# The second layer's query projection as two seven-product pairs, planned together with the feed-forward part before it

## The chip, the cores and the metric

The kernel runs on one core of a Trainium2 chip. The metric is the device time of one execution in microseconds. A core has TensorE (PE, matrix products), VectorE (DVE), ScalarE (ACT), GpSimd (POOL) and SyncE (SP, which here issues the DMAs). Each engine takes its own instructions in order, and semaphores make one wait for another.

## The reference

A trunk of two layers on 256 rows of 2048 columns, in float32. Only the parts around the change:

```python
D_MODEL = 2048; SEQ = 256; N_HEADS = 16; HEAD_DIM = 128; D_FF = 8192
...
    for l in range(N_A):                       # one layer: attention, then
        ...
        h = h + sq_relu_mlp(h, mlp_norm_g[layer], mlp_w1[layer], mlp_w2[layer])
    kv = rms_norm(h, kv_norm_g) @ kv_w         # shared keys and values
    k_sh, v_sh = jnp.split(kv, [D], axis=-1)
    k_sh = rms_norm(k_sh.reshape(B, S, H, Dh), kv_k_g)
    for l in range(N_B):                       # one layer
        u = rms_norm(h, b_norm_g[l])
        q = rms_norm((u @ b_w_q[l]).reshape(B, S, H, Dh), b_q_g[l])
        o = chunked_relbias_attention(q, k_sh, v_sh, b_rel[l])
        h = h + o.reshape(B, S, D) @ b_w_out[l]
        h = h + sq_relu_mlp(h, mlp_norm_g[layer], mlp_w1[layer], mlp_w2[layer])
```

`b_w_q` is 2048x2048: the query projection is `u @ b_w_q`, 256x2048 by 2048x2048.

## The kernel before

**Products.** A float32 product is made of three passes in a rounded type: each operand x is split into a high part hi and a rest lo = x - hi, and hi·hi, lo·hi and hi·lo are added up in PSUM (`passes`, L461, L463, L465: L461 and L463 read the weights' hi, with the activations' high and low part, L465 the weights' lo). The weights are split on the chip: a unit is a tile of 128x1024 weights, two input tiles (of 128) by 512 columns; ACT makes its hi (L217), DVE its lo (L218). There are three hi and three lo buffers, and four for the raw weights, so the splits run at most two or three units ahead of TensorE. A plain unit is 12 matmuls: two input tiles, two blocks of 128 rows, three passes.

**Panels.** An output panel is 512 columns by the 256 rows, and takes 8 units (u = 0 to 7) over the 16 input tiles. `stage` computes the first two panels side by side, and the others one after another. After each plain unit `run_fill` issues one slot of a list of side work (`fill`), to which the steps that follow from a panel are added: `add_fill` puts its first list into the next slot.

**Seven-product pairs.** In the feed-forward parts, two panels (a, the left, and b, the right) form a `Pair`. Its first four (or, in a wide pair, six) input tiles and two row blocks and two panels are taken as a 2x2 by 2x2 block product and multiplied in seven products instead of eight (`form_products`). The seven items are called "11", "T3", "T2", "T1", "21", "T4", "22" (`Form`); the names are those of the four weight blocks w11, w12, w21, w22 and of four sums of them: T3 = w22 + w12, T2 = T3 + w11, T4 = w21 + T2, T1 = w12 + w11. `bring` (L798) loads a block by DMA into a room of the tags "k" and "v"; `make` (L802, L810) makes a sum on DVE; in wide pairs `put` makes T1 and T4 by an adding DMA. `prepare` does so at set distances (units left until the pair begins), given by `when`, for ("12", "22", "21", "11", "T3", "T1"). The sums of the activations that the items "T3", "T2", "T1" and "22" need are made by `sums` (L284 to L294). An item of 1024 columns is six matmuls. In PSUM the parts are put together by copies on ACT (L890, L896, L912) and by DVE (L892 after the third item, L900 after the pair's own a2 or a3).

**The plan.** `plan_mlp` writes the order of all pairs of a feed-forward part: `Pair.plan` puts the four first items between the last three units b5, b6, b7 of the pair before, and the other three between its own units, as `own` says ("F" is an item). The feed-forward part of layer 1 has 16 pairs: for each of four chunks of 2048 hidden columns two pairs of the first and two of the second weight matrix. Its very first pair is 1024 wide with the order "early"; the others are wide.

**Around the query projection.** The residual stream h is held in SBUF by rows. When a panel n of h is done (L582), `next_x` queues: sums of squares (`rows`, L411), a turn of 32x32 blocks (L329), a DMA out to memory and back (`carry`, L339, L345) that completes the turn, and `split_turned`: scaling by the norm's gain (L305), hi (L308) and lo (L309). That gives a quarter of the projection's input, four tiles. In which slot each step stands is listed in `LONG` (this stage) and `SHORT`. The same turned rows, flipped, are later split again for the K/V projection (`again`). The queries are normed per head (`head_norm`: L538, L541, L545, L546, then L550 and L329), carried out and back, and scaled (`scale_q`, L572).

The query projection is one `stage` of four plain panels, after the feed-forward part:

```python
    turns[0] = 1 - turns[0]
    stage(xb, evs, (1 - turns[0], 2))
```

The order of instructions on DVE, ACT, TensorE and SP is the written order (`keep_order`).

Of the kernel before, what the change touches and what calls it, by code (L numbers as in the profile page):

```python
# [9 lines left out]
F32 = mybir.dt.float32  # L10
# [39 lines left out]
def trunk(ctx: ExitStack, tc: tile.TileContext, xT, xr, gs, hg, bf, wgate, w_in, w_oa, w1a, w1fa, w1sa, w2fa, w2sa,  # L50
# [69 lines left out]
    class Pair:  # L120
# [9 lines left out]

        def plan(self, rest):
            made = [self.items(f"f{i} h{i}" if self.wide else f"f{i}") for i in range(7)]
            own = {"early": "a2 F a3 F b2 F b3 a4 b4 a5 a6 a7", "wide": "a3 F b3 F a4 F b4 a5 a6 a7", "ahead": "a3 F a4 F a5 F a6 a7 b3 b4"}[self.order].split()
            plan = made[0] + rest[:1] + made[1] + rest[1:2] + made[2] + rest[2:] + made[3]
            n = 4
            for i in own:
                if i == "F":
                    plan += made[n]
                    n += 1
                else:  # L140
                    plan += self.items(i)
            return plan, self.items("b5 b6 b7")

    def plan_mlp(w1, w1f, w1s, w2f, w2s, tail):
# [12 lines left out]

        close = (7, 5, 1, 4, 3, 2)
        for c in range(NCH):
            for q in range(2):  # L160
                i = 2 * c + q
                order = "ahead" if i else "early"
                when = (25, 20, 9, 15, 10, 8) if not i else (9, 7, 1, 5, 3, 2) if i == 1 else close
                add(w1, w1f, w1s, i, WIDE1, order, when)
            for q in range(2):
                i = 2 * c + q
                add(None, w2f, w2s, i, WIDE2, "wide", close)
        plan, rest = [], [(tail, 0, u) for u in range(KT // UA - 3, KT // UA)]
# [9 lines left out]
    n_out = w_oa.shape[0] - 3  # L178
    queue(w_oa, n_out)
    tail_a = Tail(w_oa, n_out - 5)  # L180
    plan_a = plan_mlp(w1a, w1fa, w1sa, w2fa, w2sa, tail_a)
    queue(w_qb, w_qb.shape[0])
    for i in range(w_kv.shape[0]):
        units.append(w_kv[i])
    queue(w_ob, n_out)
# [163 lines left out]
    def turned(name=None):  # L349
        z = qkv.tile([P, GH * T], F32, name="z")  # L350
        return (z, qkv.tile([P, GH * T], F32, name=name, tag=name, bufs=2)) if name else z


    LONG = ((0, 1, 3, 5, 9, 10), (0, 1, 3, 5, 11, 12), (0, 1, 3, 5, 9, 10), (0, 1, 3, 5, 9, 10))
    SHORT = ((3, 1, 2, 3, 6, 7, 9, 9, 10), (4, 2, 3, 5, 10, 11, 13, 14, 22), (1, 2, 3, 4, 9, 10), (0, 0, 1, 2, 4, 5))

    def next_x(n, r2, stats, which, into, kept=None, fs=None, then=None):
        add_h = residual(n, r2)
        zt, way = [], []
        fs = fs if n < 2 else None  # L360
        at = (LONG if kept is not None else SHORT)[n]

        def use(flipped=False, which=which, into=into):
            t = zt[1].rearrange("p (i k b c) -> p k b i c", i=4, k=GH, b=NB)
            if flipped:
                t = t[:, :, :, ::-1, ::-1]
            return split_turned(t, n, which, into, fs)
# [24 lines left out]
        return f  # L392
# [409 lines left out]
    def make(p, name):  # L802
        t = p.t
        if name == "T3":
            t[name] = prob.tile([P, 9 * 3 * P], F32, name="wT3", tag="p", bufs=1) if p.order == "early" else room("bias", "wT3")
# [17 lines left out]
    def mlp(plan, x, Sx, st, last):  # L823
        base = turns[0]
        hids = [[] for _ in range(NCH)]
        Sh = [[] for _ in range(NCH)]
# [42 lines left out]
        def open_pair(p):  # L869
            m = pairs.index(p)  # L870
            c, second, r = m // 4, m % 4 >= 2, m % 2
            p.x, p.fs = (hids[c], Sh[c]) if second else (x, Sx)
            p.ps = [acc_pair(base), acc_pair(2 if p.third else 1 - base)]
            if second:
# [43 lines left out]
    xkv = []  # L918
    again = [steps(lambda n=n: kept[n](True, 2, xkv)) for n in range(NG)]
    add_fill([[], [], [st2.both], [], [st2.flip]])  # L920
# [136 lines left out]
```

## Time and profile before

| | |
|---|---|
| time, median of 3 runs | 2087.33 us (2087.27 to 2087.92) |
| the profiled execution's own time | 2087.66 us |
| its span | 2085.9 us |
| TensorE busy | 2080.1 us (100%), 9242 matmuls |
| DVE busy | 1614.3 us (77%) |
| ACT busy | 1247.4 us (60%) |
| DMA | 538.85 MB, mean 258 GB/s |

In a row of a group stand the line, the engine, the operation, output and inputs with their shapes, the count, the busy time and the mean of one in ns, and after a bar the idle time ahead of them and who ended it. In a row of the timeline stand the start and the length in us, the engine, the line, the operation, and how many instructions were merged (xN); in brackets the idle time before and who ended it. A row of a windows answer gives a stretch, its length, then busy time and count for PE, PEld, DVE, ACT and POOL, the granted clock, the DMA share and GB/s.

### The profile page before, as it was taken

What the parts mean: (1) busy time and instruction counts of PE and PEld (TensorE: products, weight loads), DVE (VectorE), ACT (ScalarE), POOL (GpSimd) and SP (SyncE); (2) the same over time, 40 slices, a digit from 0 to 9 for tenths busy, and PEclk for the clock granted to TensorE, in tenths of its full rate; (3) what the DMA queues carried; (4) which work ended last, traced back from release to release, by engine and by line L of the source; (5) the groups of instructions that cost most, each with busy time, mean ns of one, the idle gap of its engine ahead of it and who ended that gap; (6) DMA issues with size and microseconds to landing.
All of it is one profiled execution on the core that took longest, in us unless ns stands there. A gap on an engine that the chain in (4) does not pass through costs nothing.

```text
span 2085.9 us, 26322 instructions
## 1 busy us (share of the span) xinstructions
PE 2080.1 (100%) x9242; PEld 1724.1 (83%) x9242; DVE 1614.3 (77%) x1944; ACT 1247.4 (60%) x1623; POOL 110.6 (5%) x123
## 2 busy tenths in 40 slices
PE   9999999999999999999999999999999999999999
PEld 7888888888888888888888888888888888888887
DVE  6767666888788888788777577778987887888786
ACT  6545455766566566557675455456765665665664
POOL 1101000000000000000001001000000000000000
PEclk9999999999999999999999999999999999999999
DMA  8787788798798799789778777788987987997895
GB/s 287 247 257 243 224 260 267 248 284 274 237 284 270 250 281 293 219 278 300 232 238 271 221 232 240 245 261 271 274 266 254 270 282 242 288 273 246 273 289 166
DMA packets 181207, 538.85 MB, mean 258 GB/s; under 512 B 36801, under 2 KB 72017, under 8 KB 181073
## 3 DMA queue, kind: packets, MB, share of 16 engines
q1 hardware_dynamic: 171248, 484.69, 68.9%
q0 software_dynamic: 9824, 52.46, 13.6%
q8 instruction: 73, 1.20, 0.2%
q14 instruction: 62, 0.50, 0.1%
HBM read 497.20 MB, written 39.87 MB: 257 GB/s over the span
## 4 chain that ended last, share of the span: by engine, by line
PE 99%; DMA 0%; DVE 0%; SPq 0%; ACT 0%; DVEq 0%; issue 0%
PE acc L461 26%; PE acc L463 26%; PE acc L465 26%; PE s L465 6%; PE s L461 6%; PE s L463 6%; PE s L604 1%; PE po L634 1%; PE s L603 0%; PE po L635 0%; DMA raw<-in_w_in 0%; PE s L726 0%; DVE lo L218 0%; ACT hi L217 0%; DVE acc L900 0%; DVE h L582 0%
## 5 line engine op out<-in xcount | busy, mean ns | idle before, releaser
L218 DVE TENSOR_TENSOR lo<-raw,hi 128x1024 fp32r<-128x1024 f32 (+1 forms) x582 | 705.2, 1215 | 233.6 <-ACT hi L217 218.4
L217 ACT ACTIVATE hi<-raw 128x1024 fp32r<-128x1024 f32 (+1 forms) x582 | 611.2, 1051 | 273.5 <-PE acc L463 208.9
L461 PE MATMUL acc<-hi,act 128*128 128x512 f32 x2122 | 584.0, 393 | 0.8 <-ACT hi L217 0.7
L463 PE MATMUL acc<-hi,act 128*128 128x512 f32 x2122 | 575.0, 389 | 0.0
L465 PE MATMUL acc<-lo,act 128*128 128x512 f32 x2122 | 574.4, 389 | 0.0
L463 PEld LDWEIGHTS acc<-hi,act 128*128 128x128 f32 x2122 | 398.1, 188 | 83.8 <-DVE act L272 0.5
L465 PEld LDWEIGHTS acc<-lo,act 128*128 128x128 f32 x2122 | 398.3, 188 | 82.8
L461 PEld LDWEIGHTS acc<-hi,act 128*128 128x128 f32 x2122 | 396.2, 188 | 81.7 <-ACT hi L217 1.2
L217 ACT ACTIVATE hi<-w 128x1024 fp32r<-128x1024 f32 x130 | 137.2, 1056 | 106.1 <-DMA w<-in_w1fa 21.0
L218 DVE TENSOR_TENSOR lo<-w,hi 128x1024 fp32r<-128x1024 f32 x130 | 157.8, 1214 | 26.1 <-ACT hi L217 26.0
L218 DVE TENSOR_TENSOR lo<-wT,hi 128x1024 fp32r<-128x1024 f32 x94 | 114.6, 1219 | 65.3 <-ACT hi L217 65.1
L217 ACT ACTIVATE hih<-w 128x512 fp32r<-128x512 f32 x120 | 75.2, 626 | 75.2 <-PE acc L463 64.3
L217 ACT ACTIVATE hi<-wT 128x1024 fp32r<-128x1024 f32 x94 | 99.1, 1055 | 27.0 <-ACT hi L217 8.9
L461 PE MATMUL s<-hi,act 128*128 128x512 f32 x392 | 106.2, 389 | 0.0
L463 PE MATMUL s<-hi,act 128*128 128x512 f32 x392 | 106.1, 389 | 0.0
L465 PE MATMUL s<-lo,act 128*128 128x512 f32 x392 | 106.1, 389 | 0.0
L217 ACT ACTIVATE hih<-wT 128x512 fp32r<-128x512 f32 x90 | 56.4, 627 | 72.2 <-PE acc L463 60.9
L218 DVE TENSOR_TENSOR loh<-w,hih 128x512 fp32r<-128x512 f32 x120 | 82.3, 686 | 19.0 <-ACT hih L217 19.0
L463 PEld LDWEIGHTS s<-hi,act 128*128 128x128 f32 x392 | 73.6, 188 | 15.3
L465 PEld LDWEIGHTS s<-lo,act 128*128 128x128 f32 x392 | 73.6, 188 | 15.3
L461 PEld LDWEIGHTS s<-hi,act 128*128 128x128 f32 x392 | 73.5, 188 | 15.2
L218 DVE TENSOR_TENSOR loh<-wT,hih 128x512 fp32r<-128x512 f32 x90 | 62.0, 688 | 20.5 <-ACT hih L217 20.2
(213 smaller groups left out, 1901.5 us busy)
## 6 DMA issues: line engine op xcount, KB each, us to landing
raw<-in_w_in SPq DMA_DIRECT2D x96, 512.0 KB, 4.9
raw<-in_w2sa SPq DMA_DIRECT2D x80, 512.0 KB, 5.8
raw<-in_w2sb SPq DMA_DIRECT2D x80, 512.0 KB, 5.8
raw<-in_w1sa SPq DMA_DIRECT2D x70, 512.0 KB, 5.9
raw<-in_w1sb SPq DMA_DIRECT2D x70, 512.0 KB, 6.0
raw<-in_w_kv SPq DMA_DIRECT2D x64, 512.0 KB, 4.5
turn<-z SPq DMA_DIRECT2D x60, 512.0 KB, 5.0
w<-in_w2fa SPq DMA_DIRECT2D x32, 768.0 KB, 7.2
```

Source lines behind the costliest of these rows:

```text
L217: S.activation(hi[:, c], raw[:, c], AF.Copy)
L218: V.tensor_tensor(lo[:, c], raw[:, c], hi[:, c].bitcast(F32), op=ALU.subtract)
L461: TE.matmul(ps[:, cols], xh, cut(hi, j), start=first, stop=False, **kw)
L463: TE.matmul(ps[:, cols], xl, cut(hi, j), start=False, stop=False, **kw)
L465: TE.matmul(ps[:, cols], xh, cut(lo, j), start=False, stop=last, **kw)
L604: TE.matmul(s[:, P : 3 * P], q[:, a, P:T], k[:, a], start=True, stop=True)
L634: TE.matmul(po[:, :T], v[:, 0, a * P : (a + 1) * P], pT[:, :2], start=True, stop=False)
```

## The change

- The query projection becomes two more pairs at the end of the plan of layer 1's feed-forward part (`plan_mlp(..., w_qb)`, and `more` in `mlp`). Both are 1024 wide, with the new orders "query" and "", and take seven products on the first four input tiles. So the first four items of the first stand between the last three units of the feed-forward part. Their weights are laid out for that (`_cols_a(..., True)`).
- All four weight sums are made on DVE; T3 (and T2, in its place) gets a third of a new tile `query` from the pool `prob`; the other two thirds hold the turned parts three and four of the input.
- The activations' sums are made for part one (`fs=Sb`, `thirds=False`).
- `LONG` is rewritten: with fewer slots between the steps.
- The flipped parts for K/V, the row statistics and the head norms (now deferred for all groups but the first) get other slots.

```diff
@@ Pair.plan
-            own = {"early": "a2 F a3 F b2 F b3 a4 b4 a5 a6 a7", "wide": "a3 F b3 F a4 F b4 a5 a6 a7", "ahead": "a3 F a4 F a5 F a6 a7 b3 b4"}[self.order].split()
+            own = {"early": "a2 F a3 F b2 F b3 a4 b4 a5 a6 a7", "wide": "a3 F b3 F a4 F b4 a5 a6 a7", "ahead": "a3 F a4 F a5 F a6 a7 b3 b4",
+                   "query": "a2 F b2 F a3 F b3 a4 b4 a5 a6 a7", "": "a2 F a3 F a4 F a5 a6 a7 b2 b3 b4"}[self.order].split()
@@ plan_mlp
+        if more is not None:
+            for q in range(2):
+                add(more, None, None, q, (), "" if q else "query", close if q else (7, 5, 1, 4, 2, 1))
...
-    plan_a = plan_mlp(w1a, w1fa, w1sa, w2fa, w2sa, tail_a)
-    queue(w_qb, w_qb.shape[0])
+    plan_a = plan_mlp(w1a, w1fa, w1sa, w2fa, w2sa, tail_a, w_qb)
@@ next_x
-    LONG = ((0, 1, 3, 5, 9, 10), (0, 1, 3, 5, 11, 12), (0, 1, 3, 5, 9, 10), (0, 1, 3, 5, 9, 10))
+    def query_room(i):
+
+        if not query:
+            query.append(prob.tile([P, 9 * 3 * P], F32, name="query", tag="p", bufs=1))
+        return query[0][:, i * UN : i * UN + UN]
+
+    LONG = ((0, 1, 2, 4, 6, 7, 8, 9, 9), (0, 1, 2, 4, 6, 7), (0, 0, 1, 3, 5, 6), (0, 0, 1, 3, 5, 6))
...
-        fs = fs if n < 2 else None
+        fs = fs if n < 1 + thirds else None
...
-            zt.extend(turned("s" if kept is not None and n >= 2 else "q"))
+            zt.extend((turned(), query_room(n - 1)) if kept is not None and n >= 2 else turned("q"))
@@ make
         if name == "T3":
+            if p.order in ("query", ""):
+                t[name] = query_room(0)
...
@@ open_pair
+            if c == NCH:
+                p.x, p.fs, evacs = more
+                p.evac = evacs[2 * r : 2 * r + 2]
...
@@ after the plan
-    mlp(plan_a, x1, S1, st1, lambda n, r2: next_x(n, r2, st2, 3, xb, kept))
...
-    slots = {4: 0, 5: 0, 11: 1, 12: 1, 13: 2, 14: 2, 21: 3, 22: 3}
-    add_fill([[again[slots[i]]] if i in slots else [] for i in range(23)])
+    slots = {7: 0, 8: 0, 11: 1, 12: 1, 13: 2, 14: 2, 18: 3, 19: 3}
+    def next_b(n, r2):
+        f = next_x(n, r2, st2, 3, xb, kept, fs=Sb, thirds=False)
...
-                box["lq"], box["f"] = lq, head_norm(lambda: st2, z, lq, apart=(0, 2, None, None)[g])
+                box["lq"], box["f"] = lq, head_norm(lambda: st2, z, lq, apart=0 if g else None)
...
-                add_fill([[]] * (7 + (2, 4, 0, 0)[g]) + [[lambda: qs.append(scale_q(box["lq"], 1, g))]])
+                add_fill([[]] * (9 if g else 7) + [[lambda: qs.append(scale_q(box["lq"], 1, g))]])
-    turns[0] = 1 - turns[0]
-    stage(xb, evs, (1 - turns[0], 2))
+    mlp(plan_a, x1, S1, st1, next_b, (xb, Sb, evs))
```

More of the change, by code (lines that the diff above doesn't have):

```diff
@@ L142, in plan, with plan_mlp @@
             return plan, self.items("b5 b6 b7")
-    def plan_mlp(w1, w1f, w1s, w2f, w2s, tail):
+    def plan_mlp(w1, w1f, w1s, w2f, w2s, tail, more=None):
         pairs = []
@@ L351, in turned, with next_x @@
         return (z, qkv.tile([P, GH * T], F32, name=name, tag=name, bufs=2)) if name else z
-    LONG = ((0, 1, 3, 5, 9, 10), (0, 1, 3, 5, 11, 12), (0, 1, 3, 5, 9, 10), (0, 1, 3, 5, 9, 10))
+    query = []
+    def query_room(i):
[3 more added lines that the diff above has]
+    LONG = ((0, 1, 2, 4, 6, 7, 8, 9, 9), (0, 1, 2, 4, 6, 7), (0, 0, 1, 3, 5, 6), (0, 0, 1, 3, 5, 6))
     SHORT = ((3, 1, 2, 3, 6, 7, 9, 9, 10), (4, 2, 3, 5, 10, 11, 13, 14, 22), (1, 2, 3, 4, 9, 10), (0, 0, 1, 2, 4, 5))
-    def next_x(n, r2, stats, which, into, kept=None, fs=None, then=None):
+    def next_x(n, r2, stats, which, into, kept=None, fs=None, then=None, thirds=True):
         add_h = residual(n, r2)
         zt, way = [], []
-        fs = fs if n < 2 else None
+        fs = fs if n < 1 + thirds else None
         at = (LONG if kept is not None else SHORT)[n]
@@ L366, in use @@
                 t = t[:, :, :, ::-1, ::-1]
-            return split_turned(t, n, which, into, fs)
+            return split_turned(t, n, which, into, None if flipped else fs)
         def turn():
-            zt.extend(turned("s" if kept is not None and n >= 2 else "q"))
+            zt.extend((turned(), query_room(n - 1)) if kept is not None and n >= 2 else turned("q"))
             for b in range(NB):
@@ L804, in make @@
         if name == "T3":
-            t[name] = prob.tile([P, 9 * 3 * P], F32, name="wT3", tag="p", bufs=1) if p.order == "early" else room("bias", "wT3")
+            if p.order in ("query", ""):
+                t[name] = query_room(0)
+            else:
+                t[name] = prob.tile([P, 9 * 3 * P], F32, name="wT3", tag="p", bufs=1) if p.order == "early" else room("bias", "wT3")
         else:
@@ L821, in prepare, with mlp @@
                 (bring if name[0] != "T" else put if p.adds and name == "T1" else make)(p, name)
-    def mlp(plan, x, Sx, st, last):
+    def mlp(plan, x, Sx, st, last, more=None):
         base = turns[0]
@@ L871, in open_pair @@
             c, second, r = m // 4, m % 4 >= 2, m % 2
-            p.x, p.fs = (hids[c], Sh[c]) if second else (x, Sx)
+            if c < NCH:
+                p.x, p.fs = (hids[c], Sh[c]) if second else (x, Sx)
             p.ps = [acc_pair(base), acc_pair(2 if p.third else 1 - base)]
-            if second:
+            if c == NCH:
+                p.x, p.fs, evacs = more
+                p.evac = evacs[2 * r : 2 * r + 2]
+            elif second:
                 p.evac = [(last if c == NCH - 1 else residual)(2 * r + q, st.r2) for q in range(2)]
@@ L916, in trunk, with g @@
     st2, xb, kept = RowStats("b"), [], []
-    mlp(plan_a, x1, S1, st1, lambda n, r2: next_x(n, r2, st2, 3, xb, kept))
-    xkv = []
+    xkv, Sb = [], []
     again = [steps(lambda n=n: kept[n](True, 2, xkv)) for n in range(NG)]
-    add_fill([[], [], [st2.both], [], [st2.flip]])
-    slots = {4: 0, 5: 0, 11: 1, 12: 1, 13: 2, 14: 2, 21: 3, 22: 3}
-    add_fill([[again[slots[i]]] if i in slots else [] for i in range(23)])
+    slots = {7: 0, 8: 0, 11: 1, 12: 1, 13: 2, 14: 2, 18: 3, 19: 3}
+    def next_b(n, r2):
+        f = next_x(n, r2, st2, 3, xb, kept, fs=Sb, thirds=False)
+        def g(b, ps):
+            f(b, ps)
+            if (n, b) == (NG - 1, NB - 1):
+                add_fill([[], [], [st2.both], [], [st2.flip]])
+                add_fill([[again[slots[i]]] if i in slots else [] for i in range(20)])
+        return g
     qs, evs = [], []
@@ L1035 @@
         "w_kv": _cols_a(kv),
-        "w_qb": _cols_a(i["b_w_q"][0]),
+        "w_qb": _cols_a(i["b_w_q"][0], True),
         "w_ob": _cols_a(i["b_w_out"][0]),
```

## The prediction

> **What bounds the kernel now.** I read the page first: the head, the busy shares, the chain that ended last, and the costliest groups.
>
> ```profile
> span 2085.9 us, 26322 instructions
> PE 2080.1 (100%) x9242; PEld 1724.1 (83%) x9242; DVE 1614.3 (77%) x1944; ACT 1247.4 (60%) x1623; POOL 110.6 (5%) x123
> PE 99%; DMA 0%; DVE 0%; SPq 0%; ACT 0%; DVEq 0%; issue 0%
> L463 PE MATMUL acc<-hi,act 128*128 128x512 f32 x2122 | 575.0, 389 | 0.0
> ```
>
> TensorE bounds it: 100% busy, 99% of the chain. So a matmul that goes is time that goes, and any wait that TensorE gets is time that comes. I next read the timeline of TensorE through the query projection, and where this kernel, at the end of the feed-forward part before it, already lets TensorE wait.
>
> ```profile
> 1046.81 1.07 PE L461 MATMUL acc<-hi,act 128*128 128x512 f32 x4
> 1047.71 1.07 PE L463 MATMUL acc<-hi,act 128*128 128x512 f32 x4
> ...
> 1134.15 1.07 PE L461 MATMUL acc<-hi,act 128*128 128x512 f32 x4
> ...
> 1012.84 0.39 PE L465 MATMUL acc<-loh,Sh 128*128 128x512 f32 x1
> ...
> 1017.60 0.39 PE L465 MATMUL acc<-loh,act 128*128 128x512 f32 x1
> 1018.12 1.17 PE L461 MATMUL acc<-hi,act 128*128 128x512 f32 x4
> ```
>
> The stage runs from 1046.81 to 1134.15, 87.34 us for 32 units of 12 matmuls, 384: one every 0.227 us. Four start within 0.9 us (1046.81 to 1047.71) although each is shown as 389 ns long: they overlap. A unit is thus 2.72 us, a seven-product item of six matmuls 1.36 us, a pass of four 0.91 us. At 1018.12 TensorE starts 0.29 us late (1017.60 plus 0.23 would be 1017.83); the reason is below.
>
> How much room has DVE? The windows answer gives TensorE, its weight loads, DVE and ACT; the first row is the first half of the query stage, the second the first pair of layer 1's feed-forward part, which is built as the query pairs will be (1024 wide, sums added on DVE).
>
> ```profile
> 1046.81:1090.63 43.82, 43.82 (x195) 36.19 (x194) 30.23 (x34) 34.69 (x52) 0.71 (x1) 1.00 0.76 242
> 368.50:412.00 43.50, 43.50 (x193) 36.05 (x192) 34.64 (x41) 30.58 (x42) 0.00 (x0) 1.00 0.74 255
> ```
>
> DVE is at 69% in the query stage (30.23 of 43.82), and at 80% in the pair of layer 1, where TensorE has no gap: 43.50 of 43.50.
>
> **What goes: matmuls.** In each of two pairs, four units (48 matmuls) become seven items of six (42). 12 fewer x 0.227 = 2.72 us less. The reading of a row's mean instead of its starts would give 12 x 0.389 = 4.67 us. The Trainium skill (Perfetto Trace Analysis, Tensor Engine Instruction) says that TensorE's end times are estimated by the profiler and not observed; that speaks for the starts, and the sum by durations would be 1.95 us lower.
>
> **What comes: DVE work in written order.** Per pair DVE gets three more splits (L218), four sums of weights (L810), L892 and L900; once, six instructions for the sums of the input (L284 to L294). That is 24 more instructions; ACT gets 14. The shares above say that it fits on average. But DVE takes them in a fixed order, and at the start of a pair many stand together. Their pace, from start to next start, is read from the layer 1 pair:
>
> ```profile
> 362.20 0.42 DVE L284 TENSOR_TENSOR sum<-y 128x256 f32<-128x256 f32 x1
> ...
> 363.32 0.42 DVE L287 TENSOR_TENSOR sum<-y,sum 128x256 f32<-128x256 f32 x1
> ...
> 368.87 1.30 DVE L329 STREAM_TRANSPOSE z<-h 128x512 f32<-128x512 f32 x2
> 370.09 1.18 DVE L218 TENSOR_TENSOR lo<-w,hi 128x1024 fp32r<-128x1024 f32 x1
> ...
> 375.36 1.23 DVE L810 TENSOR_TENSOR wT<-wT,w 128x1024 f32<-128x1024 f32 x1
> 376.50 1.22 DVE L218 TENSOR_TENSOR lo<-raw,hi 128x1024 fp32r<-128x1024 f32 x1
> ...
> 384.67 0.69 DVE L892 SCALAR_TENSOR_TENSOR acc<-s,p 128x512 f32<-128x512 f32 x1
> 385.27 1.21 DVE L218 TENSOR_TENSOR lo<-w,hi 128x1024 fp32r<-128x1024 f32 x1
> ```
>
> A 1024-wide instruction (L218, L810, L309): 1.14. The four sums: 1.46 (362.20 to 363.32, and 0.34). L329 twice: 1.22. L892, 512 wide: 0.60, and so L294, as wide. Two more I take from the late start above, the residual L582 (1.32 for two) and L900:
>
> ```profile
> 1013.10 1.40 DVE L582 SCALAR_TENSOR_TENSOR h<-s,qm,h 128x512 f32<-128x512 f32 x2
> 1014.42 1.21 DVE L218 TENSOR_TENSOR lo<-w,hi 128x1024 fp32r<-128x1024 f32 x1
> ...
> 1016.15 1.21 DVE L218 TENSOR_TENSOR lo<-raw,hi 128x1024 fp32r<-128x1024 f32 x1
> 1017.29 0.69 DVE L900 TENSOR_TENSOR acc<-acc,p 128x512 f32<-128x512 f32 x1
> ```
>
> TensorE goes on 0.83 us after L900's start (1018.12 - 1017.29), so a DVE result is seen about 0.14 us after its end, a split 1.36 us after its start. L900's product was done at 1013.2 (1012.84 and 0.39), yet it stood behind the splits: DVE doesn't reorder. The Trainium skill (TensorE: Matmul & The Clock Gate, the table at its head) calls VectorE's queue strictly first-in first-out, and this row agrees; could it take L892 and L900 ahead, the second and fourth wait below would go.
>
> *First wait: the third item of the first pair.* Count t from the first item's start, f0; TensorE's order is f0, b5, f1, b6, f2, b7, f3, a2, f4, b2 (f0 to f6 are the items "11", "T3", "T2", "T1", "21", "T4", "22"; a and b the units of the left and right panel; b5 to b7 still the feed-forward part's). When does DVE reach f0's split? What precedes it on ACT is seen here:
>
> ```profile
> 1065.38 1.06 ACT L217 ACTIVATE hi<-raw 128x1024 fp32r<-128x1024 f32 x1 [0.53 <-PE acc L463]
> 1066.35 0.89 ACT L305 ACTIVATE y<-s,gsb 128x256 f32<-128x256 f32 x2
> 1067.28 1.06 ACT L308 ACTIVATE act<-y 128x1024 fp32r<-128x1024 f32 x1
> ...
> 1068.37 1.23 DVE L309 TENSOR_TENSOR act<-y,act 128x1024 fp32r<-128x1024 f32 x1 [0.67 <-ACT act L308]
> 1069.72 1.13 PE L463 MATMUL acc<-hi,act 128*128 128x512 f32 x4
> ```
>
> With three hi buffers, a7's L217 waits for b4's L463, which ends 0.91 + 1.07 after b4's start at t = -10.88: -8.90. Then 0.97 (L217), 0.93 (L305), 1.09 to L309 and 1.14 for it: f0's split starts at -4.8. From there DVE has eight 1024-wide instructions (splits f0, b5, f1, b6; L810 three times; L309) 9.12, sums 1.46, L294 twice 1.20, L582 1.32, L329 1.22: f2's split starts at 9.52, and TensorE has it at 10.88. It wants it after f0, b5, f1, b6 (8.16) and two passes (0.91): 9.07. Wait 1.8 us.
>
> *Second: L900 ahead of b2.* From f2's split (ends its slot at 10.66): splits b7, f3, a2, f4, b2 and L810 6.84, L892 0.60, L582 1.32, L900 to TensorE 0.83: 20.25. TensorE is there at 10.88 + 0.45 + 2.72 + 1.36 + 2.72 + 1.36 = 19.49. Wait 0.75 us, of the kind that 1018.12 shows.
>
> *Third: the third input part at a4.* ACT makes it right after b4's L217, whose buffer was a3's and is now f6's: a3's L463 ends 5.44 - 1.98 = 3.46 before a4, f6's 4.08 - 1.07 = 3.01 before it. 0.45 us later; today that split ends at 1069.60 (1068.37 and 1.23), just as a4's second pass is due (1069.72, longer than the 1.07 of others): nothing is in hand. Wait 0.45 us.
>
> *Fourth: f3 of the second pair.* Its head norm comes between. L541 with L545 and L550 with L329:
>
> ```profile
> 1089.90 0.68 DVE L541 TENSOR_REDUCE ss<-sq 128x4 f32<-128x512 f32 x1
> 1090.61 0.23 DVE L545 TENSOR_SCALAR ss<-ss,eb 128x4 f32<-128x4 f32 x1
> ...
> 1103.22 0.69 DVE L550 TENSOR_TENSOR qn<-s,ss 128x512 f32<-128x512 f32 x1
> 1103.94 0.71 DVE L329 STREAM_TRANSPOSE z<-qn 128x512 f32<-128x512 f32 x1
> 1104.62 1.22 DVE L218 TENSOR_TENSOR lo<-raw,hi 128x1024 fp32r<-128x1024 f32 x1
> ```
>
> L541 can't start before 0.8 (a7's last end 0.16, a square on ACT 0.6). Then 2 x 0.91, six 1024-wide 6.84, 2 x 1.40, L892 to TensorE 0.83: 13.1. f3, which writes the bank that L892 reads, is due at 12.24. Wait 0.85, and 0.2 for its own split behind L892.
>
> The sum of the waits is 1.8 + 0.75 + 0.45 + 1.05 = 4.05, against 2.72: **+1.3 us**. L582 doesn't wait there for TensorE, since DVE comes to it later than that. Of the loads w11 is the near one: it goes out behind a load that waits for a5's split, about 11 us before f0, and lands 4.4 to 5.5 us later (rows below); L217 of f0 has to end by -4.8, so 5.5 us would add 0.4. I take none. ACT's 14 instructions, six L217 of 1.06 and eight half as wide, some 11 us, lie in its idle fifth to third (34.69 of 43.82, 30.58 of 43.50). The K/V input parts and the norms change their places and issue what they did, rows and returns on SP's queue included; SP issues as many weight loads as before, into other rooms. The new room of the input parts was the sums' of the last hidden chunk, whose reader, the feed-forward part's last item, is done 11 us before f0 (f6, then b4, a5, a6, a7). For the waits together the bounds are nothing (the layer 1 pair at 80% shows no gap) and 4.05 with 0.4 for w11 and 0.4 for a DVE slower by one per cent (12 to 15 us of burst ahead of each of three waits). I stay near the upper end because that pair's plan has its L810 "T3" and "T1" made ten and eight units ahead, and here it is two and one: they stand inside the burst.
>
> The profiled run took 2087.66 us at a span of 2085.9; I add the sum to the median, 2087.33: **2088.6 us**.
>
> **Rivals.** *The waits are hidden*: DVE gains on ACT somewhere ahead of f0 and enters the burst 2 us sooner. For it: the layer 1 pair. Against: the order is written, and f0's split hangs on a buffer. Then only part of the waits stays, at best none: 2084.6 (2087.33 - 2.72) to 2087.
>
> *The turned input comes late* (slower). The parts three and four go out to memory and back, with two units instead of four between the return's issue and ACT's first use; while ACT waits, every L217 behind it waits.
>
> ```profile
> turn<-z SPq DMA_DIRECT2D x5, 512.0 KB, 6.6
> z<-turn SPq DMA_DIRECT2D x12, 128.0 KB, 6.3
> s<-turn SPq DMA_DIRECT2D x8, 128.0 KB, 4.0
> raw<-in_w_qb SPq DMA_DIRECT2D x27, 512.0 KB, 4.4
> raw<-in_w_kv SPq DMA_DIRECT2D x6, 512.0 KB, 5.5
> ```
>
> Part four leaves at 21.2 (L900 at 19.42, 0.60, L329 1.22), is out at 27.8, four issues and the landing, back at 33 (with 4.0) to 35.6 (with 6.3). ACT wants it ahead of a7's L217 at about 34.6, two units before a6, and has about 1 us in hand. From some 14 us for the round trip on, each us costs one; at 18 us it is 2088.6 + 4.0 = 2092.6. For it: 6.3 us. Against: the same tiles took 4.0 in this stage.
>
> *A matmul is worth its row's 389 ns*: 2087.33 - 4.67 = 2082.7 with the waits hidden. Against: the starts.
>
> **How the numbers follow.** 0.2% (4.2 us) is about what a measurement of this kernel can tell from no change: below 2083.2 is faster, above 2091.5 slower. The forecast's case (net 0 to +3) gets 0.64, hidden waits 0.22, the late input 0.11, the third rival 0.03. Faster 0.03, same 0.88, slower 0.09 (the late input reaches past 2091.5 in most of its cases). The range, 2085.2 to 2091.0, leaves out the lowest of the second case and the top of the third.
>
> **What would show it.** TensorE's instructions 9230; the two pairs' clean length 84.6 us. In the timeline a third pass (L465) of the first query pair's third item about 1.8 us late with DVE's split as releaser, b2 0.75 us late behind L900, f3 of the second pair about 0.9 us late behind L892; DVE without idle time from about 4.8 us before f0 for over 20 us. Wrong it is if DVE shows idle time inside that stretch and TensorE none, or if ACT waits there for a return from memory.

## The result and the profile after

The changed kernel takes **2091.77 us** (median of 15 executions, 2090.06 to 2093.64), the kernel before beside it 2087.66 us (15, 2087.10 to 2088.65): a ratio of 1.0020, 95% interval 1.0012 to 1.0028. It is slower by 4.1 us; the prediction had 2088.6 with 2085.2 to 2091.0, so the result lies above the range. The profiled execution of the changed kernel took 2093.03 us at a span of 2091.3. The changed file's lines stand lower: L461, L463, L465 are now L472, L474, L476 (the three passes), L217 and L218 are L220 and L221, L305 to L309 are L308 to L312, L329 is L332, L582 is L593, L810 is L824, L892 is L910, L900 is L918.

The page of the changed kernel, head, busy shares and chain:

```profile
span 2091.3 us, 26332 instructions
PE 2079.9 (99%) x9230; PEld 1719.8 (82%) x9230; DVE 1633.3 (78%) x1968; ACT 1256.7 (60%) x1637; POOL 113.6 (5%) x123
PE 93%; DMA 3%; DVE 2%; ACT 1%; issue 1%; SPq 0%; DVEq 0%; ACTq 0%
```

The 12 matmuls are gone (9242 to 9230), DVE has 24 instructions more and ACT 14, as worked out. The new thing is the chain: TensorE carried 99% of it before, now 93%, and transfers and DVE stand in it. Such a share is not time lost, but it says that what ends last is no longer TensorE's own work everywhere.

How much of the 4.1 us is made in the query stage? Take the time from the last narrow product ahead of it (1017.60 in the kernel before, a row of the prediction) to the next head norm after it, the first squares of the K/V projection. First the kernel before, then the changed one:

```profile
1155.66 1.09 ACT L538 ACTIVATE sq<-acc 128x512 f32<-128x512 f32 x2 [1.07 <-PE acc L465]
```

```profile
1018.32 0.39 PE L476 MATMUL acc<-loh,act 128*128 128x512 f32 x1
1160.00 1.09 ACT L549 ACTIVATE sq<-acc 128x512 f32<-128x512 f32 x2 [2.11 <-PE acc L476]
```

That is 138.06 us before (1155.66 - 1017.60) and 141.68 after (1160.00 - 1018.32): **+3.62 us**. With 2.72 saved, the waits in it must be some 6.3 us. TensorE's timeline shows them (start, length, then the line; the bracket is the idle time and its releaser):

```profile
1043.88 0.61 PE L474 MATMUL s<-hi,S 128*128 128x512 f32 x2
1046.31 0.74 PE L476 MATMUL s<-lo,S 128*128 128x512 f32 x2 [1.82 <-DVE lo L221]
...
1050.20 0.62 PE L474 MATMUL s<-hi,S 128*128 128x512 f32 x2
1052.16 0.72 PE L476 MATMUL s<-lo,S 128*128 128x512 f32 x2 [1.34 <-DVE lo L221]
...
1060.47 0.61 PE L476 MATMUL acc<-lo,act 128*128 128x512 f32 x2
1061.59 1.17 PE L472 MATMUL s<-hi,act 128*128 128x512 f32 x4 [0.50 <-DVE s L918]
...
1072.60 1.20 PE L472 MATMUL acc<-hi,act 128*128 128x512 f32 x4
1073.86 1.19 PE L474 MATMUL acc<-hi,act 128*128 128x512 f32 x4
1074.89 1.08 PE L476 MATMUL acc<-lo,act 128*128 128x512 f32 x4
...
1098.38 1.07 PE L476 MATMUL s<-lo,act 128*128 128x512 f32 x4
1100.16 0.70 PE L472 MATMUL acc<-hi,S 128*128 128x512 f32 x2 [0.72 <-DVE acc L910]
```

Subtract from each distance of two starts the matmuls between them at 0.227 us. The second product (T3) waits 1.98 us for its split (1046.31 - 1043.88 - 0.45), the third (T2) 1.51; with the 0.1 to 0.13 us that each start after a wait loses besides, and some 0.15 in the passes between, the two make 3.9. Then 0.67 at b2 behind L918, 0.47 at a4, 0.87 at the second pair's fourth product behind L910; with their 0.1s, b2 is 0.76, the last 1.08. The sum is 6.2 us. The wait at T3 was not forecast, the one at T2 was, with 1.8. What lies ahead of both is read in the chain of waits of that stretch, in order of time (start, us, what):

```profile
1028.45 6.85 DMA w<-in_w_qb
1035.30 0.02 issue
1035.32 0.04 ACTq L220
1035.36 0.04 issue
1035.41 1.07 ACT hi L220
1036.47 0.02 issue
1036.50 1.22 DVE lo L221
```

The weights of the first product (w11) are issued at 1028.45 and land 6.85 us later. ACT and DVE both stood idle for them:

```profile
1032.37 1.06 ACT L311 ACTIVATE act<-y 128x1024 fp32r<-128x1024 f32 x1
1035.41 1.06 ACT L220 ACTIVATE hi<-w 128x1024 fp32r<-128x1024 f32 x1 [1.98 <-DMA w<-in_w_qb]
1036.50 1.22 DVE L221 TENSOR_TENSOR lo<-w,hi 128x1024 fp32r<-128x1024 f32 x1 [1.81 <-ACT hi L220]
...
1045.03 1.22 DVE L221 TENSOR_TENSOR lo<-query,hi 128x1024 fp32r<-128x1024 f32 x1
...
1050.92 1.18 DVE L221 TENSOR_TENSOR lo<-query,hi 128x1024 fp32r<-128x1024 f32 x1
```

From 1036.50 DVE has no idle time until 1066; what starts late there stays late. So the first reading is: the burst is as long as forecast, but it starts 2 us late (the first product starts at 1039.34, so the burst begins at t = -2.84 instead of the forecast -4.8).

### The profile page after: what moved, and what is told of

It is laid out like the page before. It is cut to its first block, busy times and chain, and to the rows that moved or that the text cites. A ratio compares the mean times of both kernels' runs of the same rounds, so it can differ in the third digit from the quotient of the medians.

```text
span 2091.3 us, 26332 instructions
## 1 busy us (share of the span) xinstructions
PE 2079.9 (99%) x9230; PEld 1719.8 (82%) x9230; DVE 1633.3 (78%) x1968; ACT 1256.7 (60%) x1637; POOL 113.6 (5%) x123
## 4 chain that ended last, share of the span: by engine, by line
PE 93%; DMA 3%; DVE 2%; ACT 1%; issue 1%; SPq 0%; DVEq 0%; ACTq 0%
PE acc L474 25%; PE acc L472 25%; PE acc L476 25%; PE s L472 6%; PE s L474 6%; PE s L476 6%; DMA turn<-z 1%; DMA q<-turn 1%; DVE lo L221 1%; PE s L615 1%; PE po L645 1%; DMA raw<-in_w1b 0%; ACT hi L220 0%; PE s L614 0%; PE po L646 0%
## 5 line engine op out<-in xcount | busy, mean ns | idle before, releaser
L221 DVE TENSOR_TENSOR lo<-raw,hi 128x1024 fp32r<-128x1024 f32 (+1 forms) x574 | 695.9, 1216 | 224.5 <-ACT hi L220 209.4
L220 ACT ACTIVATE hi<-raw 128x1024 fp32r<-128x1024 f32 (+1 forms) x574 | 602.8, 1051 | 258.5 <-PE acc L474 200.7
L472 PE MATMUL acc<-hi,act 128*128 128x512 f32 x2108 | 581.1, 394 | 1.8 <-ACT hi L220 1.5
L474 PE MATMUL acc<-hi,act 128*128 128x512 f32 x2108 | 571.9, 389 | 0.1
L476 PE MATMUL acc<-lo,act 128*128 128x512 f32 x2108 | 571.1, 389 | 0.1
L474 PEld LDWEIGHTS acc<-hi,act 128*128 128x128 f32 x2108 | 395.2, 188 | 84.5 <-DVE act L312 1.5
L476 PEld LDWEIGHTS acc<-lo,act 128*128 128x128 f32 x2108 | 395.4, 188 | 82.9 <-DVE lo L221 0.7
L472 PEld LDWEIGHTS acc<-hi,act 128*128 128x128 f32 x2108 | 393.2, 188 | 83.3 <-ACT hi L220 2.3
L220 ACT ACTIVATE hi<-w 128x1024 fp32r<-128x1024 f32 x140 | 147.9, 1057 | 118.8 <-PE acc L474 23.6
L221 DVE TENSOR_TENSOR lo<-w,hi 128x1024 fp32r<-128x1024 f32 x140 | 170.1, 1215 | 36.2 <-ACT hi L220 36.0
L221 DVE TENSOR_TENSOR lo<-wT,hi 128x1024 fp32r<-128x1024 f32 x94 | 114.7, 1220 | 62.7 <-ACT hi L220 62.6
L220 ACT ACTIVATE hih<-w 128x512 fp32r<-128x512 f32 x120 | 75.2, 627 | 73.9 <-PE acc L474 62.9
L220 ACT ACTIVATE hi<-wT 128x1024 fp32r<-128x1024 f32 x94 | 99.1, 1055 | 23.0 <-PE acc L474 7.7
L472 PE MATMUL s<-hi,act 128*128 128x512 f32 x386 | 104.8, 390 | 0.5 <-DVE s L918 0.5
L474 PE MATMUL s<-hi,act 128*128 128x512 f32 x386 | 104.6, 389 | 0.0
L476 PE MATMUL s<-lo,act 128*128 128x512 f32 x386 | 104.5, 389 | 0.0
L220 ACT ACTIVATE hih<-wT 128x512 fp32r<-128x512 f32 x90 | 56.4, 627 | 68.7 <-PE acc L474 55.7
L221 DVE TENSOR_TENSOR loh<-w,hih 128x512 fp32r<-128x512 f32 x120 | 82.4, 686 | 18.7 <-ACT hih L220 18.7
L472 PEld LDWEIGHTS s<-hi,act 128*128 128x128 f32 x386 | 72.2, 188 | 15.9 <-issue 1.1
L474 PEld LDWEIGHTS s<-hi,act 128*128 128x128 f32 x386 | 72.5, 188 | 15.1
L476 PEld LDWEIGHTS s<-lo,act 128*128 128x128 f32 x386 | 72.5, 188 | 15.1
L221 DVE TENSOR_TENSOR loh<-wT,hih 128x512 fp32r<-128x512 f32 x90 | 61.9, 688 | 15.8 <-ACT hih L220 15.4
```

Of the source, the lines that this page charges most:

```text
L220: S.activation(hi[:, c], raw[:, c], AF.Copy)
L221: V.tensor_tensor(lo[:, c], raw[:, c], hi[:, c].bitcast(F32), op=ALU.subtract)
L472: TE.matmul(ps[:, cols], xh, cut(hi, j), start=first, stop=False, **kw)
L474: TE.matmul(ps[:, cols], xl, cut(hi, j), start=False, stop=False, **kw)
L476: TE.matmul(ps[:, cols], xh, cut(lo, j), start=False, stop=last, **kw)
```

## The experiments

*Theory "burst"*: DVE's work in written order, and its late start behind w11, set the waits. *Rival "input"*: the turned input's parts come late from memory. *Rival "products"*: the seven products cost more than their matmuls, by themselves. Each was run beside the kernel before, on the same chip; "stage" is the length defined above, of each run's profile, against 138.06.

| run | median us (range) | before | ratio (95%) | stage |
|---|---|---|---|---|
| the change | 2091.77 (2090.06-2093.64) | 2087.66 | 1.0020 (1.0012-1.0028) | +3.62 |
| w11_sooner | 2089.61 (2088.55-2090.68) | 2087.46 | 1.0010 (1.0001-1.0018) | +1.81 |
| t1_by_dma | 2090.22 (2089.20-2093.11) | 2087.46 | 1.0014 (1.0005-1.0024) | +1.83 |
| no_weight_sums | 2086.28 (2085.41-2088.60) | 2087.46 | 0.9995 (0.9986-1.0004) | -1.53 |
| b2_after_f5 | 2092.68 (2092.02-2094.93) | 2087.46 | 1.0027 (1.0017-1.0037) | +5.36 |
| return_sooner | 2090.97 (2089.35-2092.42) | 2087.52 | 1.0017 (1.0008-1.0026) | +3.83 |
| sums_sooner | 2090.06 (2088.65-2092.14) | 2087.52 | 1.0013 (1.0004-1.0022) | +1.73 |
| t1_t4_by_dma | 2087.47 (2085.99-2090.29) | 2087.52 | 1.0001 (0.9992-1.0010) | -0.33 |
| all_sooner | 2087.09 (2086.28-2089.32) | 2087.52 | 0.9999 (0.9990-1.0007) | -0.72 |
| w11_later | 2096.53 (2095.58-2097.39) | 2087.33 | 1.0041 (1.0029-1.0054) | +8.60 |
| t4_later | 2093.80 (2090.40-2094.78) | 2087.33 | 1.0027 (1.0018-1.0036) | +5.66 |

**w11_sooner.** The weights of the first product leave one place sooner.

```diff
-                add(more, None, None, q, (), "" if q else "query", close if q else (7, 5, 1, 4, 2, 1))
+                add(more, None, None, q, (), "" if q else "query", close if q else (7, 5, 1, 5, 2, 1))
```

> The load of w11 of the first query pair is issued one unit sooner (distance 5 instead of 4). Theory 'burst': DVE's burst at the start of the first query pair begins when f0's hi is made, and ACT waited 1.98 us for w11 to land; with the load sooner the burst starts up to 1.9 us earlier, the two waits of TensorE at the third passes of T3 and T2 (3.6 us together after the change) fall to about 1.8, and the time to about 2089.9. Rival 'input' (the turned parts three and four hold ACT): no change, 2091.8. Rival 'products' (the seven items save less than 2.72 us): no change, 2091.8.

Measured 2089.61 us. ACT no longer waits for these weights; ACT's, DVE's and TensorE's rows of this run:

```profile
1032.89 1.05 ACT L220 ACTIVATE hi<-w 128x1024 fp32r<-128x1024 f32 x1
1034.16 1.22 DVE L221 TENSOR_TENSOR lo<-w,hi 128x1024 fp32r<-128x1024 f32 x1
...
1048.58 1.18 DVE L221 TENSOR_TENSOR lo<-query,hi 128x1024 fp32r<-128x1024 f32 x1
...
1042.98 0.62 PE L472 MATMUL s<-hi,S 128*128 128x512 f32 x2
...
1046.36 1.19 PE L476 MATMUL acc<-lo,act 128*128 128x512 f32 x4
1047.74 0.74 PE L472 MATMUL s<-hi,S 128*128 128x512 f32 x2 [0.19 <-ACT s L914]
1048.31 0.62 PE L474 MATMUL s<-hi,S 128*128 128x512 f32 x2
1049.82 0.74 PE L476 MATMUL s<-lo,S 128*128 128x512 f32 x2 [0.88 <-DVE lo L221]
```

Here the prediction's working can be held against the chip with the load out of the way. The second product starts at 1042.98, so f0 at 1038.90 (4.08 earlier). f0's split is at t = -4.74 (forecast -4.8), T2's split at 9.68 (9.52), and TensorE takes it at 10.92 (10.88), 1.85 us late (1.8). That wait shows in two pieces, 0.47 ahead of the first pass, where ACT's copy L914 is late, and 1.06 ahead of the third, besides the short losses. The wait at T3 is gone. L914 is late because of the returned input: ACT stood 2.27 us at the second part's return (1039.85) and from there to L914 has no idle time. In the changed kernel it stood there for only 0.17 us, since the late weights held it first.

**w11_later.** The opposite: place 3 instead of 4 in the same line.

> The first product's weights leave one unit later than in the changed kernel (place 3 instead of 4), nothing else: the suspected cost, enlarged. Theory 'late load': in the changed kernel ACT waited 1.98 us for these weights, so nothing is in hand and each us of delay goes whole onto the start of DVE's work and from there onto the first waits; a unit is 2.72 us: 2091.8 + 2.7 = 2094.5 us, ACT's wait 4 to 5 us, the waits at the second and third product together 6 to 6.5 instead of 3.7. Theory 'burst alone' (the length of DVE's work in written order sets these waits, not when it starts): 2091.8 us, or up to 1 us more.

Measured 2096.53 us, 4.8 more than the change, where 2.7 was expected. SP's issue and ACT's row:

```profile
1031.81 0.43 SPq L811 DMA_DIRECT2D w<-in_w_qb  x1
...
1039.38 1.06 ACT L220 ACTIVATE hi<-w 128x1024 fp32r<-128x1024 f32 x1 [6.29 <-DMA w<-in_w_qb]
```

ACT gets the weights at 1039.38, 3.97 us later than in the changed kernel, although one place is a unit of 2.72. The issue went out at 1031.81 instead of 1028.45, 3.36 later, since it fell behind a third load and the input's four returns on SP's queue; the landing took another 0.6. (In this profile the stage starts 0.37 us sooner, at 1017.95; counted from there the delay is 4.34.) That delay came out whole, with about half a microsecond on top; the stage is 4.98 us longer than the change's. The waits lie elsewhere than expected: 1.95 us around the first product (1.47 of it ahead of 1040.48), 1.5 at b5, 3.0 at T3, 1.4 at b6 and nothing at T2's split. So the load theory holds and "burst alone" falls; the delay was mis-sized because a place in the plan is not a time on SP's queue.

**sums_sooner.** The input's sums one unit sooner.

```diff
-    LONG = ((0, 1, 2, 4, 6, 7, 8, 9, 9), (0, 1, 2, 4, 6, 7), (0, 0, 1, 3, 5, 6), (0, 0, 1, 3, 5, 6))
+    LONG = ((0, 1, 2, 4, 6, 7, 7, 8, 8), (0, 1, 2, 4, 6, 7), (0, 0, 1, 3, 5, 6), (0, 0, 1, 3, 5, 6))
```

> The input's sums are made one unit sooner (places 7, 8, 8 instead of 8, 9, 9), nothing else. In the changed kernel DVE stands idle for 1.8 us just ahead of the first product's split, and then works without a gap for 27 us. Theory 'burst' (the waits at the second and third product are the length of that DVE work): the first sums (1.46 us) move into the idle time, the two waits shrink together from 3.6 to 2.2 us: 2091.8 - 1.4 = 2090.4 us; waits at b2, a4 and f3 as they were. Theory 'load alone' (they are set by when the weights of the first product land): nothing changes, 2091.8 us.

Measured 2090.06 us, near the burst theory's 2090.4; "load alone" falls. The sums now run from 1034.35 to 1035.8, where DVE had been idle for the load. In this profile the weights came 1 us sooner than in the changed kernel's (ACT waited 0.95), so the profile alone would show too much; the median of 11 executions is the measure. Those range over 3.5 us, and the interval overlaps the change's (1.0012 to 1.0028), so this run supports the theory but would not carry it alone. What the rows add is that T2's wait stays at 1.50 us although the weights came sooner: from the end of L312 on, DVE's work is as long as before.

**t1_by_dma.** T1 of both pairs is added by a transfer into its tile, not by DVE.

```diff
-        G.dma_start(p.t[name][:, :WIDE], p.big[other], accum_op=ALU.add)
+        w = WIDE if p.wide else UN
+        G.dma_start(p.t[name][:, :w], p.big[other], accum_op=ALU.add)
...
-                (bring if name[0] != "T" else put if p.adds and name == "T1" else make)(p, name)
+                (bring if name[0] != "T" else put if (p.adds or p.order in ("query", "")) and name == "T1" else make)(p, name)
```

> T1 = w12 + w11 of both query pairs is made by an adding DMA, as in the wide pairs, instead of by DVE. Theory 'burst': 1.14 us leaves the burst ahead of T2's split in the first pair, so TensorE's waits there fall by 1.1 us, and up to 0.9 us at f3 of the second pair: 2090.6 to 2089.8, unless the adding DMA lands after T1's split wants it. Rivals 'input' and 'products': no change, 2091.8.

Measured 2090.22 us, within the expected 2089.8 to 2090.6. One sum of 1.14 us less in the burst; the wait at T3 is gone, and one of 1.25 us at T2's first pass, for ACT's copy, has come up. This profile's w11 wait was only 0.90, which does a part of it. What held ACT ahead of that copy is again the second part's return, with no idle time from there to the copy:

```profile
1039.95 0.91 ACT L308 ACTIVATE y<-q,gsb 128x256 f32<-128x256 f32 x2 [2.09 <-DMA q<-turn]
```

The wait in the second pair, expected to shrink by up to 0.9, is as long as before (0.99 ahead of its fourth product): there the burst starts with the head norm, and T1's sum stands ahead of that.

**no_weight_sums.** `make` returns one of the two summands' tiles for T1 to T4.

```diff
         t = p.t
+        if p.order in ("query", ""):
+            t[name] = t[{"T1": "12", "T2": "22", "T3": "22", "T4": "11"}[name]]
+            return
```

> Leaves out the four sums of weights of both query pairs (the items multiply w22, w22, w12 and w11 in place of T3, T2, T1 and T4); everything else, all matmuls too, is the changed kernel's. Theory 'burst': 3.4 us leave the burst ahead of T2's split and 1.1 more ahead of b2, 2.3 ahead of f3 of the second pair; of 6.2 us of waits about 1 stays (a4's 0.5 and a rest of the first), so 2087.7 - 2.7 + 1 = 2086.0, between 2085 and 2087. Rival 'products': not below 2087.7. Rival 'input': at least 2089.

Measured 2086.28 us. With the four sums of each pair off DVE, the stage is 1.53 us shorter than before: the 2.72 us less 1.2 of waits that are left (0.5 at T2's first pass, 0.47 at a4, and small ones). The medians alone can't tell this from no change (0.9986 to 1.0004), but against the kernel before, this run lies 5.3 us under the change, and 2.72 us less 1.2 of waits is all that its stage shows. So the saving is real and "products" falls: the seven products cost nothing but what their preparation costs.

**b2_after_f5.** b2 a unit later in the plan, to give L918 time.

```diff
-                   "query": "a2 F b2 F a3 F b3 a4 b4 a5 a6 a7", ...
+                   "query": "a2 F a3 F b2 F b3 a4 b4 a5 a6 a7", ...
```

> The first query pair's own order is the one of layer 1's first pair: b2 stands after f5 and a3 instead of right after f4, so L918 has 4.1 us more until its reader. Theory 'burst': the wait of 0.76 us at b2 goes, the others stay: 2091.0. Rivals 'input' and 'products': no change, 2091.8.

A miss: 2092.68 us instead of 2091.0. The wait at b2 went, as it should; a new one of 2.0 us came at a6. ACT's row, and the landings of what was issued from 1066 to 1077:

```profile
1078.08 0.91 ACT L308 ACTIVATE y<-query,gsb 128x256 f32<-128x256 f32 x2 [3.25 <-DMA query<-turn]
...
raw<-in_w_qb SPq DMA_DIRECT2D x5, 512.0 KB, 7.7
w<-in_w_qb SPq DMA_DIRECT2D x2, 512.0 KB, 7.9
query<-turn SPq DMA_DIRECT2D x4, 128.0 KB, 7.0
```

The same window and the same rows in the changed kernel:

```profile
1076.76 0.91 ACT L308 ACTIVATE y<-query,gsb 128x256 f32<-128x256 f32 x2 [0.60 <-DMA query<-turn]
...
raw<-in_w_qb SPq DMA_DIRECT2D x4, 512.0 KB, 4.7
w<-in_w_qb SPq DMA_DIRECT2D x2, 512.0 KB, 6.3
query<-turn SPq DMA_DIRECT2D x4, 128.0 KB, 4.4
```

This is the prediction's rival of the late input: part four's return landed 7.0 us after its issue instead of 4.4, and there was nothing in hand. In the changed kernel itself it cost ACT 0.60 us and TensorE nothing that can be seen.

**return_sooner.** b2_after_f5 again, with that return asked for one unit sooner.

```diff
-    LONG = (..., (0, 0, 1, 3, 5, 6), (0, 0, 1, 3, 5, 6))
+    LONG = (..., (0, 0, 1, 3, 5, 6), (0, 0, 1, 2, 5, 6))
```

> The order of b2_after_f5 again, and the fourth input part's return from memory issued one unit sooner (its third place 2 instead of 3). Theory 'late return': in b2_after_f5 the new wait of 1.66 and 0.35 us at the fifth unit's successor is that return alone, issued at 1069.24 though the part had left at 1062.11 and 3.9 us later was out (1066.0). One unit sooner the issue comes about 3 us earlier, the 3.25 us that ACT waited for it go, and both TensorE waits with them: 2092.7 - 2.0 = 2090.7 us, the first wait (2.3) still there. Theory 'crowded queues': the return took 7.0 us instead of 4.4 because it stood among weight loads; sooner it stands behind as many, the wait stays, 2092 to 2093 us.

Measured 2090.97 us: 1.7 less than b2_after_f5, where 2.0 was expected. The wait at a6 is gone and the return lands in 3.6 us:

```profile
query<-turn SPq DMA_DIRECT2D x4, 128.0 KB, 3.6
```

So the miss was the return, and "crowded queues" (a long landing wherever it is issued) falls for it. What the order itself brought, the wait at b2, did not come out as time: this profile has 2.62 and 1.51 at T3 and T2 and 0.99 behind L910. There the first weights landed late again (ACT waited 2.62).

**t4_later.** T4 made right ahead of its split.

```diff
-            if done == 1 and not f.wide:
+            if done == (3 if getattr(f, "order", 0) in ("query", "") else 1) and not f.wide:
                 make(f, "T4")
```

> The sum T4 of both query pairs is made two units later, right ahead of its own split, nothing else. Theory 'written order': it then no longer stands ahead of the instructions that release b2 (L918) and the fourth product of the second pair (L910); at 1.14 us it is longer than either wait (0.76 and 1.08), so both go whole: 2091.8 - 1.84 = 2089.9 us, the first wait as it was. Theory 'throughput': DVE's work up to the sixth product's split is the same, so the waits come back there and at the units behind it: 2091 to 2092 us.

The second miss: 2093.80 us instead of 2089.9. The waits at b2 and behind L910 both went, with T4's sum alone moved. Two others took their place, as ACT's rows show:

```profile
1061.62 1.06 ACT L220 ACTIVATE hi<-w 128x1024 fp32r<-128x1024 f32 x1 [3.88 <-DVE w L824]
...
1078.19 0.91 ACT L308 ACTIVATE y<-query,gsb 128x256 f32<-128x256 f32 x2 [3.23 <-DMA query<-turn]
```

ACT reaches the rounding of T4 long before DVE makes the sum, and waits 3.88 us for it with three further L220 behind; TensorE then waits 0.7 us around the sixth product in the first pair and 1.4 in the second. And part four is late as in b2_after_f5 (landing 6.6 us), 2.1 us at a6. I had moved one DVE instruction and looked at DVE's queue alone; the one that stood waiting was ACT's. The Trainium skill (Perfetto Trace Analysis, Tensor Engine Instruction) says in passing that ACT and DVE take their instructions strictly first-in first-out, and the 3.88 us agree.

**t1_t4_by_dma.** t1_by_dma, with T4 added by a transfer too, and w11 sooner.

```diff
-            elif form.name == "T2" and half:
+            elif form.name == "T2" and (half or form.pair.order in ("query", "")):
                 put(form.pair, "T4")
...
-            if done == 1 and not f.wide:
+            if done == 1 and not f.wide and f.order not in ("query", ""):
                 make(f, "T4")
```

> T1 and T4 of both pairs are made by an adding transfer instead of on DVE (two of the four sums), and the weights of the first product leave one unit sooner. Theory 'burst': T4's sum (1.14 us on DVE) stands ahead of the instruction that releases b2 and ahead of the one that releases the fourth product of the second pair, whose waits are 0.65 and 0.9 to 1.1: both go. The first wait becomes what it was without the sums, 0.5 to 1 us on ACT's copies at the third product's first pass. With a4's 0.47 that makes 1.0 to 1.5 us of waits against 2.72 us saved: 2086.3 to 2087.3, say 2086.8 us. Theory 'transfers crowd': the adding transfers land 6.5 us after their issue in t1_by_dma, and T4's is wanted some 8 us after the third product's split; two more of them in the busy queues make them, the first weights or the returned input late, and the sixth product waits: 2088 to 2091 us.

Measured 2087.47 us, 0.2 above the expected 2086.3 to 2087.3: no difference from before, 4.3 us less than the change. The stage is 0.33 us shorter than before. The waits at T3, at b2 and behind L910 are gone; 0.8 is left at T2 (in pieces), 0.48 at a4, 0.4 near 1077, 0.56 at the second pair's third product. "Transfers crowd" falls: T4 comes in time.

**all_sooner.** That kernel, and in it `LONG = ((0, 1, 2, 4, 6, 7, 7, 8, 8), (0, 0, 1, 3, 6, 7), (0, 0, 1, 3, 5, 5), (0, 0, 1, 2, 5, 6))`.

> As t1_t4_by_dma, with the input's parts sooner: sums one unit sooner (7, 8, 8), part two leaves and is asked back one unit sooner (0, 0, 1, 3, 6, 7), both halves of part three made at the fifth unit (0, 0, 1, 3, 5, 5), part four asked back one unit sooner (0, 0, 1, 2, 5, 6). Theory 'burst': a4's wait (0.47) goes, since ACT makes part three ahead of the weights that wait for a buffer; ACT's wait of 2.3 us for part two in w11_sooner goes, and with it up to half of the wait at the third product's first pass: 2086.8 - 0.5 to 1.0, say 2086.0 us, below both kernels. Theory 'transfers crowd': the returns and sums that come sooner meet the weight loads of the first product; a wait on SP's queue delays those, 2087 to 2090 us.

Measured 2087.09 us, 1.1 above the expected 2086.0; 0.4 us under the kernel before, which the interval (0.9990 to 1.0007) doesn't tell from nothing. The wait at a4 is gone, and so is ACT's wait for the second part, with TensorE's at T2's first pass. What is left in the first pair is one wait:

```profile
1047.03 0.61 PE L474 MATMUL s<-hi,S 128*128 128x512 f32 x2
1048.20 0.73 PE L476 MATMUL s<-lo,S 128*128 128x512 f32 x2 [0.55 <-DVE lo L221]
```

It is the third product's split again, 0.72 us. This is the best version found: the waits are 2.0 us against 2.72 saved.

## Why the prediction was wrong, point by point

- **What bounds it, and the saving: right.** 12 x 0.227 = 2.72 us; no_weight_sums shows it, as nothing but the waits eats it. The 389 ns rival is out.
- **The first wait: this term was mis-sized, 1.8 taken, 3.9 measured.** Its working was right but for one step, "I take none" for w11. The burst's start and the third product's split fell within 0.2 us of the forecast once the load was out of the way (w11_sooner), and the wait was 1.85. The step that failed is the landing, 4.4 to 5.5 us by the rows of the kernel before; it was 6.85. In the seven profiles with the issue at this place it was 5.8 to 7.5 us (ACT's wait was 0.90 to 2.62). The prediction's own price, 0.4 at 5.5 us and one for one beyond, gives 1.8 at 6.9.
- **Why the landing was mis-sized.** The rows that I used are medians of the loads that the kernel before issues from 1046.8 to 1134.2, in its query stage. w11 goes out 18 us ahead of that. The two weight loads that the kernel before itself issues there, at 1027.4 and 1029.2, already took 6.0 and 6.6 us (one at 1025.8 only 3.5), and no engine stood waiting for them:

```profile
raw<-in_w2sa SPq DMA_DIRECT2D x1, 512.0 KB, 6.0
...
raw<-in_w2sa SPq DMA_DIRECT2D x1, 512.0 KB, 6.6
```

  By the prediction's own price such landings add 0.9 to 1.5 us instead of none, an estimate of 2089.5 to 2090.1 us. Is the rest the change's own traffic? The windows around the issue (busy PE, PEld, DVE, ACT, POOL, then PE's clock, the share of the DMA engines, GB/s), before and then after:

```profile
1020.00:1028.00 8.00, 8.00 (x37) 6.59 (x37) 6.38 (x8) 4.77 (x5) 0.00 (x0) 1.00 0.63 180
1028.00:1036.00 8.00, 8.00 (x37) 6.64 (x36) 3.60 (x3) 2.90 (x3) 0.00 (x0) 1.00 0.91 295
```

```profile
1020.00:1028.00 8.00, 8.00 (x37) 6.61 (x36) 6.99 (x8) 4.29 (x6) 0.00 (x0) 1.00 0.96 289
1028.00:1036.00 8.00, 8.00 (x37) 6.62 (x36) 3.72 (x4) 4.91 (x8) 0.00 (x0) 1.00 0.93 300
```

  The pairs bring their weights in ahead of the first product (three w loads in 1018 to 1036, none before), so in the 8 us ahead of the issue the DMA engines are 0.96 busy instead of 0.63. But in the 8 us in which w11 is under way they are 0.93 busy, and were 0.91 before. So a landing of over 6 us there is not new, and whether the change's own loads made it longer was not tested; what sets it between 5.8 and 7.5 us stays open. The Trainium skill (DMA: Bandwidth & Descriptors, Anatomy of one DMA) has 2.0 us and the bytes at 436 GB/s for a single transfer issued by GpSimd, an estimate of 3.2 us for 512 KB; no load of this stretch lands so soon, and the formula has no term for those beside it.
- **The second, third and fourth wait: right.** 0.75, 0.45 and 1.05 forecast; 0.76, 0.47 and 1.08 measured, behind the instructions named. T4's sum is the one that matters for the second and the fourth: t4_later, which moves it alone, and t1_t4_by_dma, which takes it off DVE, both remove them, while w11_sooner and t1_by_dma leave them (0.64 and 0.66, 0.93 and 0.99). That shows the written order as their cause. The third has no run of its own; it is gone in all_sooner, where several steps move.
- **The net.** 1.3 us forecast, 3.62 in the stage; 2.1 of the 2.3 between them is the first wait. The profiled execution shows 5.4 more in its span: beside the 3.62, 0.72 lies ahead of the stage (1018.32 against 1017.60) and 1.06 behind it (from the end row to the span's end 931.3, before 930.2). In the other ten profiles the part behind is 929.8 to 930.8, so this is scatter of single executions. The medians stand 0.4 us above what the stages say, on average over the eleven comparisons (-0.4 to 0.9). That is not a loss outside the stage: the profiled execution's own time less its stage is 1949.6 us before and 1949.0 to 1949.9 in the ten experiments. The profile shows one execution, and in seven of the ten that one is 0.2 to 1.0 us under the median of its kernel.
- **The rivals.** Hidden waits: no, all four stand in TensorE's timeline. The late input: it cost TensorE nothing in the change, but it was close. The prediction has it cost from some 14 us on, from the fourth part's leaving to ACT's use. That took 14.1 us in the change (1062.67 to 1076.76) and 16.0 in b2_after_f5, where the wait was 2.0. In t4_later, where the part left 1.7 us sooner than there, it took 17.8 and the wait was 2.1. The prediction didn't look at the second part, whose return held ACT in w11_sooner and t1_by_dma. The forecast's range ended at 2091.0 because w11 entered it with 0.4 at most.
- **What would show it.** DVE without idle time for over 20 us: yes, 30 us. But its start was 2 us later than the -4.8 that the prediction named, and that was the sign to look for. ACT did stand at returns in that stretch and behind it (0.17 and 0.60 us), and TensorE lost nothing by it.

## What to carry to other kernels

When a change makes a load land just in time, look up what the loads issued at that very place of the profile took, even if nobody waited for them there, and price it at the longest of them, not at the median of another stretch (here 6.6 against 4.4 to 5.5 us; 6.85 came). A burst of work in written order passes on a late start whole, so ask first when it starts, and only then how long it is. And when an instruction is moved later on one engine, look at who waits for it on the others' queues: ACT, standing at a sum that DVE made later, took back a little more than DVE gained (2.1 us at the two sixth products, against 1.84).

## What the runs showed that I had not expected

- The median landing of a 512 KB load was 4.3 us in one window of this stage (four loads) and 8.2 in another (two loads; both in w11_later, from 1066 and from 1031), and moving an issue by one place moved it by 3.4 us, not by 2.72.
- 128 KB returns landed in 3.6 us when issued at 1066.65 and in 7.0 when issued at 1069.24, behind almost the same loads. Why, the runs don't tell.
- The two adding transfers of 512 KB in t1_by_dma, issued by GpSimd, landed in 7.1 and 5.8 us; nothing in TensorE's timeline of that run waits for one.
